# Weight tiles with even and odd columns in separate halves, streamed in turn by the matmuls

## The chip, the core and the metric

The kernel runs on one core of one Trainium2 chip. A core has a matrix engine (PE), which reads both operands from on-chip memory (SBUF, 128 partitions) and writes to PSUM, and four more engines: DVE (VectorE), ACT (ScalarE), POOL (GpSimd) and SP (SyncE, which here only issues DMAs). Each runs its own list of instructions in order; semaphores join them. The metric is the time of one execution in microseconds of device time (us); lower is better.

## The reference

Two layers of a decoder trunk on 256 tokens of width 1024, batch 1, all in float32. Each layer is a SwiGLU block of inner width 2816, a mixer of three gated branches (short convolution, sparse attention, attention to 256 memory tokens), and a second SwiGLU block, each between two RMS norms:

```python
def swiglu(h, w_in, w_out):
    a, b = jnp.split(h @ w_in, 2, axis=-1)
    return (jax.nn.silu(a) * b) @ w_out

for l in range(DEPTH):
    h = rms_norm(x, ffn1_norm_pre[l])
    x = x + 0.5 * rms_norm(swiglu(h, ffn1_w_in[l], ffn1_w_out[l]), ffn1_norm_post[l])
    h = rms_norm(x, mix_norm_pre[l])
    y = token_mixer(h, mem, cos, sin, ...)
    x = x + rms_norm(y, mix_norm_post[l])
    h = rms_norm(x, ffn2_norm_pre[l])
    x = x + 0.5 * rms_norm(swiglu(h, ffn2_w_in[l], ffn2_w_out[l]), ffn2_norm_post[l])
```

What matters here is that nearly all of the work is a product of a 128-token block of activations with a large float32 weight matrix: `w_in` (1024 x 5632), `w_out` (2816 x 1024), the mixer's input projection (1024 x 6424) and its smaller matrices.

## The kernel before

The tokens are two blocks of 128 (`stream(0)` and `stream(1)`), and both walk through the same list of steps, the second a few steps behind. The weights come from memory once, in units of up to 512 KB: 1024 float32 words on each of 128 partitions (128 rows by 1024 columns, or two blocks of rows by 512, or four by 256). A unit takes three steps before a matmul can use it:

- `load` (line 244) issues a DMA from SP into one of 4 tiles `raw`.
- `split_unit` (line 280) makes two tiles of it, out of 8 pairs: ACT rounds `raw` to the matrix engine's type float32r and writes `whi` (line 286), and DVE subtracts, `wlo = raw - whi` (line 287). `prefetch` (line 293) calls it up to 4 steps ahead of the use.
- the matmuls take three products for each block of 128 rows: `whi` with the high part of the activations, `wlo` with the high part, and `whi` with the low part. The activations are the stationary operand (`lhsT`, loaded by LDWEIGHTS, 128 columns), and the weights are the moving operand (`rhs`), which streams through the array: 512 columns in most matmuls.

The moving operand is a plain slice of the tile, 512 neighbouring words on each partition. These places use it: `product` (line 356, the SwiGLU input in two banks), `mm3` (lines 344 to 346) through `product2` (mixer, branches, memory, and the tail of the SwiGLU input) and through `output` (line 528), and `compress` (lines 956 and 958, 256 columns). `mm3` is also called with operands that are no weight units (`mem_attention`, `compress`).

`view(ap, off, dims)` (line 104) builds an access pattern by hand: a list of [step, count] pairs in words, the outermost first, the partition left as it is.

In the profile `acc`, `y` and `br` are PSUM banks, `hThi`/`hTlo`, `turnhi`/`turnlo` and `mThi`/`mTlo` are high and low parts of activations. The order on each engine is a fixed list that the program's walk writes out; no table is touched here.

Of the kernel before, what the change touches and what calls it, by code (L numbers as in the profile page):

```python
# [103 lines left out]
def view(ap, off, dims):  # L104
    if isinstance(ap, Nothing):
        return ap
    return bass.AP(tensor=ap.tensor, offset=ap.offset + off, ap=[list(ap.ap[0])] + [list(d) for d in dims])


def f32(ap):  # L110
    return ap.bitcast(F32)
# [19 lines left out]
def program(tc, nc, pools, a, out, plan):  # L131
# [18 lines left out]
    def bank(name):  # L150
        return psa.tile([P, 512], F32, name=name, tag="a")
# [4 lines left out]
    def gtile(name, dt=F32):  # L156
        return gp.tile([P, 1024], dt, name=name, tag="g")
# [17 lines left out]
    def pinned(ins):  # L175
        if first_steps[0] and not dry:
            tc.keep_in_program_order(ins)
# [3 lines left out]
    first = consts.tile([16, P], F32, name="first")  # L181
    nc.scalar.dma_start(first, a[PRE[0]].rearrange("l (k p) -> (l k) p", p=P))
    for half in range(2):
        sl = slice(half * 512, (half + 1) * 512)
# [45 lines left out]
    def unit(key, parts):  # L230
        hi, lo = ask("w", key, parts)
        later(0, lambda: drop("w", key))
        return hi, lo
# [46 lines left out]
    def split_unit(between=None):  # L280
        item, raw, n = splits.pop(0)
        free["w"] -= 1
        hi = wp.tile([P, 1024], F32R, name="whi")
        lo = wp.tile([P, 1024], F32R, name="wlo")
        for c0, c1 in ((0, n),) if between is None else ((0, n // 2), (n // 2, n)):
            pinned(nc.scalar.copy(hi[:, c0:c1], raw[:, c0:c1]))  # L286
            pinned(nc.vector.tensor_sub(lo[:, c0:c1], raw[:, c0:c1], f32(hi[:, c0:c1])))  # L287
            if c0 == 0 and between is not None:
                between()
        ready[item[2]] = [hi, lo]  # L290
        free["raw"] += 1

    def prefetch():
        if dry:
            return
        ahead = AHEAD if now[0] > RAMP else 1
        while splits and splits[0][0][0] <= now[0] + ahead and free["w"] > 0:
            split_unit()
        if now[0] == 0 and not prologue:
            prologue.append(True)  # L300
            load(loads.pop(0), (nc.sync, nc.scalar))
            load(loads.pop(0))
            nc.sync.dma_start(x[1], a["x"][0, P:2 * P, :])
        room = {"raw": True, "g": True}
        for item in list(loads):
            if item[0] > now[0] + LOADS or not any(room.values()):
                break
            kind = "g" if item[1] == "g" else "raw"
            room[kind] = room[kind] and free[kind] > 0
            if room[kind]:  # L310
                load(item)
                loads.remove(item)

    def fetch(key):
        while key not in ready:
            if splits and (splits[0][0][2] == key or free["raw"] == 0):
                split_unit()
            else:
                item = loads.pop(0)
                if item[1] == "g" and item[2] != key:  # L320
                    raise RuntimeError(f"no room for {key} before {item[2]}")
                load(item)
                if item[1] != "g":
                    continue
# [14 lines left out]
    if not dry:  # L339
        loads.extend(plan)  # L340
        left.update({item[2]: item[4] for item in plan})

    def mm3(ps, xh, xl, wh, wl, start, stop, skip=False):
        nc.tensor.matmul(ps, lhsT=xh, rhs=wh, start=start, stop=False, skip_group_check=skip)  # L344
        nc.tensor.matmul(ps, lhsT=xh, rhs=wl, start=False, stop=False, skip_group_check=skip)  # L345
        nc.tensor.matmul(ps, lhsT=xl, rhs=wh, start=False, stop=stop, skip_group_check=skip)  # L346

    def product(hT, name, l, cols):
        ps = [bank("acc") for _ in cols]
        for k in range(8):  # L350
            parts = [(0, -1, name, l, k, 1, cols[0][0], cols[0][1])]
            hi, lo = unit((name, l, cols[0][0], k), parts)
            for i, (x2, w) in enumerate(((0, hi), (1, hi), (0, lo))):
                for j, p in enumerate(ps):
                    n = cols[j][1]
                    pinned(nc.tensor.matmul(p[:, :n], lhsT=hT[x2][:, k], rhs=w[:, j * n:(j + 1) * n],  # L356
                                            start=(k == 0 and i == 0), stop=(k == 7 and i == 2)))
            yield 0
        return ps

    def product2(ps, x2, hi, lo, n, k0, first, last):
        for kk in range(2):
            k = k0 + kk
            mm3(ps[:, :n], x2[0][:, k], x2[1][:, k], hi[:, kk * n:(kk + 1) * n], lo[:, kk * n:(kk + 1) * n],
                first and kk == 0, last and kk == 1)

    def halves(hT, name, l, parts):
        ps = bank("acc")
        width = sum(n for _, n in parts)
        for u in range(4):  # L370
            hi, lo = unit((name, l, parts[0][0], u), [(i * n, width, name, l, 2 * u, 2, c, n)
                                                      for i, (c, n) in enumerate(parts)])
            product2(ps, hT, hi, lo, width, 2 * u, u == 0, u == 3)
            yield 0
        return ps
# [70 lines left out]
    def prenorm(src, name, l, warm=False):  # L446
# [18 lines left out]
        if warm and splits:  # L465
            pts = []
            for half in range(2):
                pts.append(transpose4(src, half * 512))
                keep_clock(WARM[1 + half])
            gained(0, pts[0])  # L470
            split_unit(lambda: halved(0))
            split_unit()
            gained(1, pts[1])
            halved(1)
        else:
            for half in range(2):
                gained(half, transpose4(src, half * 512))
            for half in range(2):
                halved(half)
# [36 lines left out]
    def output(y, name, l, count, lhs, between=None):  # L516
        steps = [[(k, 0), (k, 1)] for k in range(count)]
        if TAIL:
            steps[-TAIL:] = [[(k, 0)] for k in range(count - TAIL, count)]
            steps[-1] += [(k, 1) for k in range(count - TAIL, count)]  # L520
        for n, step in enumerate(steps):
            if between is not None:
                between(n)
            for k, i in step:
                hi, lo = unit((name, l, k), [(0, 0, name, l, k, 1, 0, 1024)])
                sl = slice(i * 512, (i + 1) * 512)
                xh, xl = lhs(k)
                mm3(y[i], xh, xl, hi[:, sl], lo[:, sl], k == 0, k == count - 1)
            yield 0


    def ffn(t, l, which):
# [15 lines left out]
        for j in range(5):  # L548
            pa, pb = yield from product(hT, w_in, l, [(j * 512, 512), (DFF + j * 512, 512)])
            gate(j, 512, pa, pb)  # L550
# [7 lines left out]
        def lhs(k):  # L558
            c = (k % 8) * P
            return [v[:, c:c + P] for v in gT[k // 8]]  # L560

        yield from output(y, w_out, l, 22, lhs, between)
        yield from postnorm(y, t, (f"ffn{which}_norm_post", l, t), 0.5, which == 2 and l == DEPTH - 1)

# [365 lines left out]
    def compress(l, i):  # L930
# [13 lines left out]
        FHL = gtile("FHL", F32R)  # L944
# [4 lines left out]
        z = bank("z")  # L949
        w1 = f"cmp_{nm}_w1"  # L950
        for u in range(4):
            hi, lo = unit((w1, l, u), [(0, 256, w1, l, 4 * u, 4, 0, 256)])
            for mm in range(4):
                m = 4 * u + mm
                c = mm * 256
                nc.tensor.matmul(z[0:64, 0:256], lhsT=FHL[:, m * 64:(m + 1) * 64], rhs=hi[:, c:c + 256],  # L956
                                 start=(m == 0), stop=False, skip_group_check=True)
                nc.tensor.matmul(z[0:32, 0:256], lhsT=FHL[:, m * 64:m * 64 + 32], rhs=lo[:, c:c + 256],  # L958
                                 start=False, stop=(m == 15), skip_group_check=True)
            yield 1  # L960
        nc.scalar.copy(zc[0:64], z[0:64, 0:256])
# [17 lines left out]
        if i == 0:  # L979
# [11 lines left out]
            ps = bank("kc")  # L991
            for ht in range(2):
                h2, l2 = wh[:, ht].rearrange("p a d -> p (a d)"), wl[:, ht].rearrange("p a d -> p (a d)")
                mm3(ps[:, 0:32], h2, l2, gh[:, ht], gl[:, ht], ht == 0, ht == 1)
# [3 lines left out]
        else:  # L998
# [11 lines left out]
            ps = bank("vc")  # L1010
# [204 lines left out]
    def mixer(t, l):  # L1215
# [11 lines left out]
        def squeeze():  # L1227
            for i in range(2):
                add(("cmp", l), compress(l, i))
# [68 lines left out]
        def between(k):  # L1298
            if k == SECOND:
                transpose_half(1)  # L1300

        yield from output(y, "w_mix_out", l, 8, lambda k: (mT[0][:, k], mT[1][:, k]), between)
        yield from postnorm(y, t, ("mix_norm_post", l, t), 1.0)

# [73 lines left out]
```

## Time and profile before

| | |
|---|---|
| median of 3 runs (lowest to highest) | 1254.22 us (1254.11 to 1254.84) |
| span of the profiled execution, first to last instruction | 1252.2 us |
| instructions | 16623 |
| DMA, mean over the span | 229 GB/s, 286.85 MB |

The profile shows one execution of the program. The span leaves out what lies before the first instruction and after the last one; the profiled execution's own time is not listed apart from the three runs, whose median is 2.0 us above its span. Busy times of PE overlap, since a matmul's end is modelled and the next one starts before it; what a matmul costs in a dense stretch is therefore read from start to start in the timeline and not from its duration. DVE and ACT rows can be read as they stand.

### The profile page before, as it was taken

What the parts mean: (1) busy time and instruction counts of PE and PEld (TensorE: products, weight loads), DVE (VectorE), ACT (ScalarE), POOL (GpSimd) and SP (SyncE); (2) the same over time, 40 slices, a digit from 0 to 9 for tenths busy, and PEclk for the clock granted to TensorE, in tenths of its full rate; (3) what the DMA queues carried; (4) which work ended last, traced back from release to release, by engine and by line L of the source; (5) the groups of instructions that cost most, each with busy time, mean ns of one, the idle gap of its engine ahead of it and who ended that gap; (6) DMA issues with size and microseconds to landing.
All of it is one profiled execution on the core that took longest, in us unless ns stands there. A gap on an engine that the chain in (4) does not pass through costs nothing.

```text
span 1252.2 us, 16623 instructions
## 1 busy us (share of the span) xinstructions
PE 1239.9 (99%) x5775; PEld 1027.1 (82%) x5775; DVE 911.3 (73%) x1160; ACT 729.5 (58%) x1146; POOL 209.6 (17%) x413
## 2 busy tenths in 40 slices
PE   8999999999999999999999999999999999999997
PEld 6888888888888888888888888878888888888886
DVE  7766766888988686666576676678899976757752
ACT  6545545887866454544464555569868744545541
POOL 3011601401120011011011014023022200110110
PEclk9999999999999999999999999999999999999999
DMA  7878876777578757776857788757667877577871
GB/s 254 261 244 260 280 250 221 215 238 217 182 264 252 219 179 210 247 255 218 260 177 224 237 269 295 246 177 245 213 185 236 281 223 218 180 241 219 257 244 70
DMA packets 133907, 286.85 MB, mean 229 GB/s; under 512 B 11872, under 2 KB 30976, under 8 KB 133824
## 3 DMA queue, kind: packets, MB, share of 16 engines
q1 hardware_dynamic: 117984, 238.78, 60.6%
q0 software_dynamic: 15520, 46.49, 11.3%
q8 instruction: 45, 0.74, 0.2%
q10 hardware_dynamic: 320, 0.53, 0.1%
q14 instruction: 38, 0.31, 0.1%
HBM read 261.64 MB, written 24.12 MB: 228 GB/s over the span
## 4 chain that ended last, share of the span: by engine, by line
PE 93%; DVE 2%; DMA 1%; ACT 1%; issue 1%; POOL 1%; SPq 0%; DVEq 0%; POOLq 0%; ACTq 0%
PE acc L356 35%; PE acc L346 9%; PE acc L344 9%; PE acc L345 9%; PE y L345 7%; PE y L346 7%; PE y L344 7%; PE pt L388 2%; PE br L344 2%; PE br L345 2%; PE br L346 2%; DMA x<-in_x_dram 1%; PE z L958 1%; PE s L917 1%; PE z L956 1%
## 5 line engine op out<-in xcount | busy, mean ns | idle before, releaser
L287 DVE TENSOR_TENSOR wlo<-raw,whi 128x1024 fp32r<-128x1024 f32 (+2 forms) x441 | 532.1, 1213 | 244.8 <-ACT whi L286 240.8
L286 ACT CAST whi<-raw 128x1024 fp32r<-128x1024 f32 (+2 forms) x441 | 456.4, 1043 | 362.5 <-PE acc L356 182.0
L356 PE MATMUL acc<-wlo,hThi 128*128 128x512 f32 x640 | 198.4, 390 | 0.0
L356 PE MATMUL acc<-whi,hThi 128*128 128x512 f32 x640 | 197.9, 390 | 0.5 <-ACT whi L286 0.5
L356 PE MATMUL acc<-whi,hTlo 128*128 128x512 f32 x640 | 197.2, 389 | 0.0
L344 PE MATMUL acc<-whi,hThi 128*128 128x512 f32 (+1 forms) x480 | 188.2, 392 | 0.4 <-ACT hThi L462 0.4
L345 PE MATMUL acc<-wlo,hThi 128*128 128x512 f32 (+1 forms) x480 | 184.8, 385 | 0.0
L346 PE MATMUL acc<-whi,hTlo 128*128 128x512 f32 (+1 forms) x480 | 184.6, 385 | 0.2
L403 POOL DMA_DIRECT2D there<-blocks x184 | 101.2, 556 | 492.3 <-DVE blocks L398 407.5
L356 PEld LDWEIGHTS acc<-whi,hThi 128*128 128x128 f32 x640 | 119.7, 188 | 25.7 <-ACT whi L286 0.8
L356 PEld LDWEIGHTS acc<-whi,hTlo 128*128 128x128 f32 x640 | 120.0, 188 | 25.2 <-DVE hTlo L463 0.3
L356 PEld LDWEIGHTS acc<-wlo,hThi 128*128 128x128 f32 x640 | 120.0, 188 | 25.2 <-DVE wlo L287 0.4
L346 PE MATMUL y<-whi,turnlo 128*128 128x512 f32 x352 | 137.3, 390 | 0.0
L345 PE MATMUL y<-wlo,turnhi 128*128 128x512 f32 x352 | 137.2, 390 | 0.0
L344 PE MATMUL y<-whi,turnhi 128*128 128x512 f32 x352 | 137.1, 389 | 0.0
L346 PEld LDWEIGHTS acc<-whi,hTlo 128*128 128x128 f32 x480 | 90.1, 188 | 18.7 <-DVE hTlo L463 0.6
L344 PEld LDWEIGHTS acc<-whi,hThi 128*128 128x128 f32 x480 | 90.3, 188 | 17.1 <-ACT hThi L462 1.3
L345 PEld LDWEIGHTS acc<-wlo,hThi 128*128 128x128 f32 x480 | 90.4, 188 | 15.0
L344 PEld LDWEIGHTS y<-whi,turnhi 128*128 128x128 f32 x352 | 66.1, 188 | 13.8
L346 PEld LDWEIGHTS y<-whi,turnlo 128*128 128x128 f32 x352 | 66.1, 188 | 13.6
L345 PEld LDWEIGHTS y<-wlo,turnhi 128*128 128x128 f32 x352 | 66.1, 188 | 13.6
L424 DVE TENSOR_TENSOR turnlo<-moved,turnhi 128x1024 fp32r<-128x1024 f32 (+1 forms) x42 | 49.2, 1171 | 33.1 <-ACT turnhi L423 33.0
(294 smaller groups left out, 1451.4 us busy)
## 6 DMA issues: line engine op xcount, KB each, us to landing
raw<-in_ffn_w_in_dram SPq DMA_DIRECT2D x159, 512.0 KB, 4.8
raw<-in_w_mix_in_dram SPq DMA_DIRECT2D x96, 512.0 KB, 4.7
raw<-in_ffn_w_out_dram SPq DMA_DIRECT2D x88, 512.0 KB, 4.6
there<-blocks POOLq DMA_DIRECT2D x152, 128.0 KB, 4.4
moved<-there POOLq DMA_DIRECT2D x38, 512.0 KB, 5.2
raw<-in_ffn_w_in_dram SPq DMA_DIRECT2D x33, 256.0 KB, 4.1
raw<-in_w_mem_kv_dram SPq DMA_DIRECT2D x16, 512.0 KB, 4.7
raw<-in_w_mix_out_dram SPq DMA_DIRECT2D x16, 512.0 KB, 4.0
```

The costliest lines, as they stand in the source:

```text
L286: pinned(nc.scalar.copy(hi[:, c0:c1], raw[:, c0:c1]))
L287: pinned(nc.vector.tensor_sub(lo[:, c0:c1], raw[:, c0:c1], f32(hi[:, c0:c1])))
L344: nc.tensor.matmul(ps, lhsT=xh, rhs=wh, start=start, stop=False, skip_group_check=skip)
L345: nc.tensor.matmul(ps, lhsT=xh, rhs=wl, start=False, stop=False, skip_group_check=skip)
L346: nc.tensor.matmul(ps, lhsT=xl, rhs=wh, start=False, stop=stop, skip_group_check=skip)
L356: pinned(nc.tensor.matmul(p[:, :n], lhsT=hT[x2][:, k], rhs=w[:, j * n:(j + 1) * n], start=(k == 0 and i == 0), stop=(k == 7 and i == 2)))
L388: pinned(nc.tensor.transpose(pt[:, j * P:(j + 1) * P], src[:, c0 + j * P:c0 + (j + 1) * P], ident))
L403: nc.gpsimd.dma_start(there[:, q * f:(q + 1) * f].rearrange("(p j) f -> j p f", j=32), blocks[q * 32:(q + 1) * 32, :n].rearrange("j (p f) ...
L424: nc.vector.tensor_sub(lv, mv, f32(hv))
L917: nc.tensor.matmul(s3[:, i], lhsT=QT[:, g * 4 + u * 2 + i], rhs=KT[j][:, var * 2 + g], start=(i == 0 and j == 0), stop=(i == 1 and j == 1) ...
L956: nc.tensor.matmul(z[0:64, 0:256], lhsT=FHL[:, m * 64:(m + 1) * 64], rhs=hi[:, c:c + 256], start=(m == 0), stop=False, skip_group_check=True)
L958: nc.tensor.matmul(z[0:32, 0:256], lhsT=FHL[:, m * 64:m * 64 + 32], rhs=lo[:, c:c + 256], start=False, stop=(m == 15), skip_group_check=True)
```

## The change

A helper `moving` builds a pattern that takes one word from the lower half of a 1024-word tile, then the word 512 further on, then the next of the lower half, and so on. `split_unit` reads `raw` with a step of two words: first the even columns, which it writes to the lower half of `whi` and `wlo`, then the odd columns, which go to the upper half. The matmuls that have weight units as moving operand read them through `moving`, so the columns come out in the same order as before. A new `mm3w` wraps `mm3` for them; matmuls of other operands stay as they are. The number of instructions, their order and their waits are the same on all five engines.

```diff
+def moving(w, c, n):
+    return view(w, c // 2, [[1, n // 2], [512, 2]])
...
         for c0, c1 in ((0, n),) if between is None else ((0, n // 2), (n // 2, n)):
-            pinned(nc.scalar.copy(hi[:, c0:c1], raw[:, c0:c1]))
-            pinned(nc.vector.tensor_sub(lo[:, c0:c1], raw[:, c0:c1], f32(hi[:, c0:c1])))
+            source = view(raw, c0, [[1, 2], [2, (c1 - c0) // 2]])
+            h2, l2 = (view(v, c0 // 2, [[512, 2], [1, (c1 - c0) // 2]]) for v in (hi, lo))
+            pinned(nc.scalar.copy(h2, source))
+            pinned(nc.vector.tensor_sub(l2, source, f32(h2)))
...
+    def mm3w(ps, xh, xl, hi, lo, c, n, start, stop):
+        mm3(ps, xh, xl, moving(hi, c, n), moving(lo, c, n), start, stop)
...
-                    pinned(nc.tensor.matmul(p[:, :n], lhsT=hT[x2][:, k], rhs=w[:, j * n:(j + 1) * n],
+                    pinned(nc.tensor.matmul(p[:, :n], lhsT=hT[x2][:, k], rhs=moving(w, j * n, n),
...
-            mm3(ps[:, :n], x2[0][:, k], x2[1][:, k], hi[:, kk * n:(kk + 1) * n], lo[:, kk * n:(kk + 1) * n],
-                first and kk == 0, last and kk == 1)
+            mm3w(ps[:, :n], x2[0][:, k], x2[1][:, k], hi, lo, kk * n, n, first and kk == 0, last and kk == 1)
...
-                sl = slice(i * 512, (i + 1) * 512)
                 xh, xl = lhs(k)
-                mm3(y[i], xh, xl, hi[:, sl], lo[:, sl], k == 0, k == count - 1)
+                mm3w(y[i], xh, xl, hi, lo, i * 512, 512, k == 0, k == count - 1)
...
-                nc.tensor.matmul(z[0:64, 0:256], lhsT=FHL[:, m * 64:(m + 1) * 64], rhs=hi[:, c:c + 256],
+                nc.tensor.matmul(z[0:64, 0:256], lhsT=FHL[:, m * 64:(m + 1) * 64], rhs=moving(hi, c, 256),
...
-                nc.tensor.matmul(z[0:32, 0:256], lhsT=FHL[:, m * 64:m * 64 + 32], rhs=lo[:, c:c + 256],
+                nc.tensor.matmul(z[0:32, 0:256], lhsT=FHL[:, m * 64:m * 64 + 32], rhs=moving(lo, c, 256),
```

## The prediction, made before the changed kernel was run

> **What bounds the kernel now.** I began with the page: busy shares, the slices of the span, the chain that ended last.
>
> ```profile
> PE 1239.9 (99%) x5775; PEld 1027.1 (82%) x5775; DVE 911.3 (73%) x1160; ACT 729.5 (58%) x1146; POOL 209.6 (17%) x413
> PEclk9999999999999999999999999999999999999999
> PE 93%; DVE 2%; DMA 1%; ACT 1%; issue 1%; POOL 1%; SPq 0%; DVEq 0%; POOLq 0%; ACTq 0%
> ```
>
> The matrix engine is busy for 99% of the 1252.2 us span, at full granted clock in every slice, and the chain is 93% PE. No wait is left to remove; the time is the number of matmuls times their spacing. The spacing is in the timeline of PE, here a stretch of the SwiGLU output (start, duration, instruction):
>
> ```profile
> 599.43 0.39 PE L344 MATMUL y<-whi,turnhi 128*128 128x512 f32 x1
> 599.66 0.39 PE L345 MATMUL y<-wlo,turnhi 128*128 128x512 f32 x1
> ...
> 611.90 0.39 PE L345 MATMUL y<-wlo,turnhi 128*128 128x512 f32 x1
> ```
>
> From 599.43 to 611.90 there are 55 spacings: 12.47 / 55 = 0.2267 us for 512 columns, 0.443 ns a column. The listed 390 ns is latency and overlaps. The count of 512-column matmuls that stream weights comes from the groups, first of the page and then of the groups kept apart by shape:
>
> ```profile
> L356 PE MATMUL acc<-whi,hThi 128*128 128x512 f32 x640 | 197.9, 390 | 0.5 <-ACT whi L286 0.5
> L344 PE MATMUL y<-whi,turnhi 128*128 128x512 f32 x352 | 137.1, 389 | 0.0
> ```
>
> ```profile
> L344 PE MATMUL acc<-whi,hThi 128*128 128x512 f32 x448 | 178.6, 399 | 0.4 <-ACT hThi L462 0.4
> L344 PE MATMUL y<-whi,mThi 128*128 128x512 f32 x64 | 25.3, 396 | 0.0
> L344 PE MATMUL acc<-whi,mThi 128*128 128x512 f32 x64 | 24.9, 389 | 0.0
> L344 PE MATMUL br<-whi,ynsa 128*128 128x512 f32 x32 | 12.6, 395 | 0.0
> ```
>
> Each group stands for three products: 3 x (640 + 352 + 448 + 64 + 64 + 3 x 32) = 4992, the last term being the three branches. At 0.2267 us they fill 1132 us, 90% of the span. So one nanosecond of spacing is worth 5.0 us, and whatever the new pattern does to the stream decides the case.
>
> **The stream: is there anything to gain?** I look for a second point on the line of spacing against columns. Matmuls of 256 columns with 128 columns of weights:
>
> ```profile
> 322.90 0.28 PE L1122 MATMUL om<-turnhi,vm 128*128 128x256 f32 x1
> ...
> 324.34 0.40 PE L344 MATMUL acc<-whi,hThi 128*128 128x512 f32 x1
> ```
>
> ```profile
> 325.73 0.28 PE L917 MATMUL s<-KTh,QT 128*128 128x256 f32 x1
> 325.84 0.28 PE L917 MATMUL s<-KTl,QT 128*128 128x256 f32 x1
> 325.96 0.28 PE L917 MATMUL s<-KTh,QT 128*128 128x256 f32 x1
> ```
>
> Twelve matmuls of L1122 take 1.44 us, 120 ns each, so the second 256 columns of a 512-column matmul cost 226.7 - 120 = 106.7 ns, 0.417 ns a column against the mean of 0.443. At that rate alone 512 columns are 213.3 ns, 13.4 ns less than now. That is the most the rows allow a better stream to gain. Whether the 13.4 ns belongs to the words or to each matmul is what the rows of L917 bear on: the first of those starts only 0.11 us before the next, so 256 columns can pass in 113 ns or so, half of 227. A fixed 13 ns for each matmul would have forbidden that. So I read the excess as a pause that comes every so many words of a contiguous float32r stream, and such a pause is something that another order of words can remove. Two half-tiles in turn make two streams, each with twice the time per word. For a loss there are rows too, taken up with the rivals.
>
> [...]
>
> **The split: what the step of two costs.** 441 units go through one ACT and one DVE instruction each, whose input now has a step of two words and whose output is two runs of 512. The rows:
>
> ```profile
> L287 DVE TENSOR_TENSOR wlo<-raw,whi 128x1024 fp32r<-128x1024 f32 x431 | 524.8, 1225 | 243.6 <-ACT whi L286 239.7
> L286 ACT CAST whi<-raw 128x1024 fp32r<-128x1024 f32 x431 | 450.2, 1052 | 360.1 <-PE acc L356 182.0 <-PE y L346 79.3 <-PE acc L346 52.5
> L424 DVE TENSOR_TENSOR turnlo<-moved,turnhi 128x1024 fp32r<-128x1024 f32 x34 | 41.6, 1222 | 20.3 <-ACT turnhi L423 20.2
> L463 DVE TENSOR_TENSOR hTlo<-hf,hThi 128x512 fp32r<-128x512 f32 x24 | 15.9, 687 | 0.6 <-ACT hThi L462 0.5
> L942 DVE TENSOR_TENSOR F<-G,smallT 128x240 f32<-128x240 f32 x8 | 4.3, 583 | 0.0
> ```
>
> L424 reads its first input in runs of 32 words with jumps between them and costs 1222 ns against 1225: jumps as such are free. L942 reads its first input with a step of 16 words. From 512 and 1024 columns (687 and 1225 ns) a contiguous column costs 1.05 ns and an instruction 149 ns, so 240 columns would be 401 ns; 583 is 182 more, 0.76 ns a column. So the two ends for the split are 0 and 1024 x 0.76 = 776 ns an instruction, for DVE 441 x 0.776 = 342 us in all. ACT has no row with a step; I take the same two ends. I choose 0, because a step of two is one doubling from a run and three from the step of 16. At this value the cover isn't even needed: in front of the splits DVE idles 243.6 us for ACT, and ACT 360.1 us mostly for PE to release a pair. If the price were the upper end, that cover holds in the SwiGLU stages only (rival C).
>
> [...]
>
> **What faster matmuls bring late.** The stages differ, in busy time of PE, PEld, DVE, ACT, POOL per 100 us:
>
> ```profile
> 200.00:300.00 100.00, 99.56 (x540) 84.14 (x539) 84.78 (x137) 80.83 (x175) 23.23 (x41) 1.00 0.70 215
> 300.00:400.00 100.00, 99.89 (x481) 82.77 (x480) 89.38 (x142) 72.90 (x147) 18.10 (x36) 1.00 0.71 226
> 500.00:600.00 100.00, 100.00 (x443) 82.81 (x442) 64.67 (x63) 47.30 (x51) 13.97 (x26) 1.00 0.75 239
> 800.00:900.00 100.00, 99.57 (x525) 83.84 (x525) 79.28 (x112) 75.12 (x152) 21.05 (x37) 1.00 0.71 224
> 900.00:1000.00 100.00, 99.27 (x496) 83.01 (x495) 90.94 (x163) 77.61 (x170) 22.33 (x42) 1.00 0.72 225
> ```
>
> In the SwiGLU stages (500 to 600) DVE and ACT have a third and more to spare, and DMA is at 0.75 of its engines' time; 5% more speed asks 0.79. In the mixers DVE is at 85 to 91%. The full gain would be 66.9 / 1252.2, 5.3 us in 100, which puts DVE at 94 to 96% in two of the windows, where a queue of dependent steps starts to show. I count nothing of the gain in those two (300 to 400 and 900 to 1000): 2 x 5.3 = 11 us given back. The ends for this term are 0 and four windows, 21 us.
>
> **The sum.** Profiled span 1252.2. Stream of the 512-column matmuls: -4992 x 13.4 ns = -66.9. The 128 matmuls of 256 columns in `compress` and the 96 of 280 gain at most half as much each, 224 x 7 ns = -1.6. Split: 0. Given back in the mixers: +11. That is 1194.7; with the 2.0 us by which the median of the runs (1254.22) stands above the span, 1196.7: **1197 us**. The likeliest case's own range is from 1186 (nothing given back) to 1222 (half of the stream's gain, 1252.2 - 34.3 + 2.0 = 1220, and a little for the split).
>
> **Rivals.** A is the forecast.
>
> B, the pause stays: the 13.4 ns is spent between matmuls (change of weights), or alternation pauses as often as a contiguous stream does. Then nothing moves and the change doesn't do what it could: 1254 us. For it: the straight line through 120 and 226.7 has just such a fixed part. Against it: the 0.11 us of L917.
>
> C, the split pays the step: DVE at 776 ns more for each unit. The DVE time of the splits alone in the mixer windows:
>
> ```profile
> 200.00:300.00 100.00, 45.53 (x39) 1.00 0.70 215
> 300.00:400.00 100.00, 35.72 (x30) 1.00 0.71 226
> 800.00:900.00 100.00, 46.77 (x40) 1.00 0.71 224
> 900.00:1000.00 100.00, 34.96 (x29) 1.00 0.72 225
> ```
>
> 39, 30, 40 and 29 splits add 30.3, 23.3, 31.0 and 22.5 us, so DVE needs 115, 113, 110 and 113 us in each 100: 51 us over, and DVE is the bound there. With an unchanged stream that is 1305 us; with A's stream, whose gain then counts only outside these windows (850 of 1252 us, 46 us), 1259. Slower either way. For it: L942. Against it: its step is 16, not 2.
>
> D, the stream itself stalls, and the change is much slower. The place is the PE's read of the moving operand: if it fetches neighbouring words together and uses both, then an order that leaves a neighbour behind with every column halves what a fetch yields. Two words a fetch means twice the spacing, 453 ns, +226.7 ns x 4992 = +1132 us: 2386 us. With the extra that L942 shows on DVE, 0.76 ns a column, it is 512 x 0.76 = 389 ns each, +1942 us: 3196 us. It decides from the first nanosecond that a column costs above 0.443. For it: L942 shows that SBUF reads of single words can cost 1.81 ns a column, four times what PE takes now. Against it: L942 never comes back to a neighbour, while here each half is read word by word in order, and every neighbour is used two columns later, if the reader holds two places at once.
>
> [...]
>
> **How the numbers follow.** Chances: A 0.52, B 0.16, C 0.12, D 0.20. A leads because the excess over 0.417 ns looks like one of words and because two ordered streams aren't single-word hops. D is as large as it is because no row shows the pattern. The range takes in A, B and C, from 1184 to 1312, and leaves out D, whose price is far off. A measurement here tells about 0.2%, 2.5 us, from no change: faster is A, 0.52; within is B, 0.16; slower is C and D, 0.32.
>
> **What would show it.** A: in the changed profile the 55 spacings of such a stretch are 213 to 216 ns, L286 and L287 stay at 1052 and 1225 ns, and PE shows its first idle time in the mixers, with ACT or DVE as releaser. B: 227 again. C: L287 near 2000 ns, DVE at full in the mixers, PE waiting for `wlo`. D: spacings of 450 ns and more with PE still at 99% and DVE idle. I am wrong most plainly if the spacing rises, since every other term is small beside it.

## The result, and the profile after

| | before | changed |
|---|---|---|
| median (lowest to highest), 4 runs each | 1254.16 us (1253.99 to 1254.84) | 1265.59 us (1259.27 to 1269.44) |
| ratio to before, 95% interval | | 1.0085 (1.0057 to 1.0113) |
| span of the profiled execution | 1252.2 us | 1257.6 us |
| mean granted PE clock of that execution | 0.998 | 0.992 |

The changed kernel is slower by 0.9%. The profiled execution is the fastest of its four, so the profile shows 5.4 of the 11.4 us between the medians. The page of the changed kernel, busy times and granted clock:

```profile
PE 1197.1 (95%) x5775; PEld 1035.6 (82%) x5775; DVE 1018.1 (81%) x1160; ACT 930.1 (74%) x1146; POOL 214.8 (17%) x413
PEclk9999989999999999999999999999999999999999
```

PE is busy 42.8 us less than before (1239.9), and idle for 1257.6 - 1197.1 = 60.5 us where it was 12.3: 48.2 us more. Two large terms nearly cancel. DVE and ACT together do 307 us more. The timeline of PE in a dense stretch of the changed kernel (start, duration, instruction):

```profile
544.81 0.38 PE L365 MATMUL acc<-whi,hThi 128*128 128x512 f32 x1
...
556.68 0.60 PE L365 MATMUL acc<-whi,hTlo 128*128 128x512 f32 x2
```

Between these two starts lie 55 spacings: 11.87 / 55 = 0.2158 us each, where it was 0.2267. So the stream gained 10.9 ns a matmul, 54 us over 4992 of them. The groups of the changed kernel by shape (busy, mean ns, idle time before them) show where it went:

```profile
L292 ACT CAST whi<-raw 128x1024 fp32r<-128x1024 f32 x431 | 656.7, 1546 | 165.8 <-PE acc L365 67.6 <-PE acc L355 20.9 <-DMA raw<-in_ffn_w_in_dram 20.7
L293 DVE TENSOR_TENSOR wlo<-raw,whi 128x1024 fp32r<-128x1024 f32 x431 | 639.4, 1496 | 148.4 <-ACT whi L292 145.9 <-PE acc L365 1.6
L431 ACT CAST turnhi<-moved 128x1024 fp32r<-128x1024 f32 x34 | 35.9, 1055 | 33.5 <-DMA moved<-there 33.3
```

The copy costs 1546 ns where it was 1052 (+494), the subtraction 1496 where it was 1225 (+271), in the 431 units of 1024 columns. A copy of the same size with other operands, L431, still costs about what it did (1055, 1046 before). What PE waited for in the changed kernel (total us, times, longest):

```profile
PE pt L396 <- DVE x L519: 7.6, 10, 1.0
PE pt L396 <- DVE v L1145: 7.0, 4, 2.6
PE acc L353 <- ACT mThi L673: 6.9, 3, 5.3
PE zt L972 <- ACT zc L968: 4.2, 2, 2.1
PE br L353 <- DVE gth L1298: 3.8, 2, 3.3
...
PE acc L365 <- DVE wlo L293: 0.3, 1, 0.3
```

Almost nothing waits for the weight tiles themselves (0.3 us for `wlo`). PE waits for other short work of DVE and ACT, which share their queues with the splits: the residual, the convolution's product, scores, gates. That it is the splits that hold these up is read from the order of the queues; a run below, with the same stream and cheaper splits, shows it better. The longest wait, 5.3 us for `mThi`, has a DMA in its chain: DVE waited up to 4.3 us for the tile `moved` before it. The windows of the changed kernel (busy time of PE, PEld, DVE, ACT, POOL, then clock, DMA share and GB/s) say where:

```profile
100.00:200.00 100.00, 92.14 (x409) 79.59 (x408) 72.24 (x63) 63.48 (x55) 29.22 (x52) 0.95 0.76 254
200.00:300.00 100.00, 90.31 (x503) 78.22 (x502) 83.47 (x116) 87.28 (x165) 21.58 (x36) 1.00 0.67 206
300.00:400.00 100.00, 94.74 (x485) 81.91 (x484) 95.00 (x155) 83.62 (x150) 22.12 (x42) 1.00 0.71 220
500.00:600.00 100.00, 100.00 (x465) 87.70 (x464) 78.96 (x68) 67.86 (x52) 16.54 (x30) 1.00 0.77 249
800.00:900.00 100.00, 93.73 (x500) 81.16 (x499) 80.61 (x96) 84.15 (x129) 22.16 (x37) 0.98 0.70 217
900.00:1000.00 100.00, 91.54 (x485) 80.32 (x484) 92.74 (x163) 84.75 (x176) 17.96 (x33) 1.00 0.67 207
```

In the SwiGLU stage from 500 to 600 the plan holds: PE is full and issues 465 matmuls where it issued 443. In the four mixer windows PE is at 90 to 95%: 29.7 us of idle time, where it was 1.7. From 100 to 200 the granted clock is 0.95 beside 8 us of idle time; before it was 1.00 in every such window. In steps of 5 us, two stretches of idle time there and the clock behind them (the same columns):

```profile
145.00:150.00 5.00, 2.41 (x11) 1.76 (x11) 3.12 (x5) 4.95 (x8) 3.80 (x7) 0.94 0.45 146
150.00:155.00 5.00, 5.00 (x18) 4.16 (x17) 4.11 (x5) 2.24 (x2) 4.74 (x8) 0.72 0.92 325
175.00:180.00 5.00, 0.78 (x2) 0.69 (x3) 3.13 (x3) 1.04 (x1) 0.00 (x0) 0.67 0.29 109
180.00:185.00 5.00, 5.00 (x17) 4.08 (x16) 0.95 (x2) 1.91 (x2) 0.00 (x0) 0.65 0.32 105
```

PE passes 18 and 17 matmuls in the full step right after the gap, at clocks of 0.72 and 0.65, and 25 in the dense steps around it. How long a gap it takes is not settled by this trace: from 265 to 270 PE is busy for 3.19 of the 5 us, and the clock is 1.00 there and in the full step behind it; from 880 to 885 it is busy for 2.76, and the clock is 0.83 there and in the step behind it. Over the span, 0.998 - 0.992 is 0.006 x 1257.6, by estimate at most 8 us, since some of it falls on idle time. The four runs move with it: 1259.3 us at 0.992, 1265.3 and 1265.9 at 0.988, 1269.4 at 0.987. The stream's 54.4 us less, 48.2 us more of idle time and these 8 us add up to 2 us more; the spans differ by 5.4, so some 4 us stay unexplained.

### The profile page after: what moved, and what is told of

Same layout as the page of the kernel before. It is cut to its first block, busy times and chain, and to the rows that moved or that the text cites. A ratio compares the mean times of both kernels' runs of the same rounds, so it can differ in the third digit from the quotient of the medians.

```text
span 1257.6 us, 16623 instructions
## 1 busy us (share of the span) xinstructions
PE 1197.1 (95%) x5775; PEld 1035.6 (82%) x5775; DVE 1018.1 (81%) x1160; ACT 930.1 (74%) x1146; POOL 214.8 (17%) x413
## 3 DMA queue, kind: packets, MB, share of 16 engines
q0 software_dynamic: 15520, 46.49, 11.4%
## 5 line engine op out<-in xcount | busy, mean ns | idle before, releaser
L292 ACT CAST whi<-raw 128x1024 fp32r<-128x1024 f32 (+2 forms) x441 | 665.3, 1531 | 167.8 <-PE acc L365 67.6
L293 DVE TENSOR_TENSOR wlo<-raw,whi 128x1024 fp32r<-128x1024 f32 (+2 forms) x441 | 647.5, 1481 | 149.9 <-ACT whi L292 147.4
L365 PE MATMUL acc<-whi,hThi 128*128 128x512 f32 x640 | 191.7, 381 | 2.1 <-DVE wide L551 1.7
L365 PE MATMUL acc<-wlo,hThi 128*128 128x512 f32 x640 | 191.9, 380 | 0.3 <-DVE wlo L293 0.3
L365 PE MATMUL acc<-whi,hTlo 128*128 128x512 f32 x640 | 190.8, 380 | 0.9 <-DVE hTlo L471 0.9
L353 PE MATMUL acc<-whi,hThi 128*128 128x512 f32 (+1 forms) x480 | 183.4, 382 | 0.7 <-ACT hThi L470 0.7
L355 PE MATMUL acc<-whi,hTlo 128*128 128x512 f32 (+1 forms) x480 | 179.9, 375 | 0.5 <-DVE hTlo L471 0.5
L354 PE MATMUL acc<-wlo,hThi 128*128 128x512 f32 (+1 forms) x480 | 179.8, 375 | 0.0
L355 PE MATMUL y<-whi,turnlo 128*128 128x512 f32 x352 | 134.6, 382 | 0.0
L431 ACT CAST turnhi<-moved 128x1024 fp32r<-128x1024 f32 (+1 forms) x42 | 42.5, 1013 | 58.8 <-DMA moved<-there 55.8
```

Of the source, the lines that this page charges most:

```text
L292: pinned(nc.scalar.copy(h2, source))
L293: pinned(nc.vector.tensor_sub(l2, source, f32(h2)))
L365: pinned(nc.tensor.matmul(p[:, :n], lhsT=hT[x2][:, k], rhs=moving(w, j * n, n), start=(k == 0 and i == 0), stop=(k == 7 and i == 2)))
L431: nc.scalar.copy(hv, mv)
```

## The experiments

The theory after the result was that the stream gains and the step of two costs the copies, each by itself. The first two runs take the change apart. Both feed the matmuls columns in another order and so compute other numbers, with the same instructions and sizes.

**The stream alone.** The split of before, the matmuls of the change (in the few units of 560 columns the halves are 280 words apart):

```diff
-            source = view(raw, c0, [[1, 2], [2, (c1 - c0) // 2]])
-            h2, l2 = (view(v, c0 // 2, [[512, 2], [1, (c1 - c0) // 2]]) for v in (hi, lo))
-            pinned(nc.scalar.copy(h2, source))
-            pinned(nc.vector.tensor_sub(l2, source, f32(h2)))
+            pinned(nc.scalar.copy(hi[:, c0:c1], raw[:, c0:c1]))
+            pinned(nc.vector.tensor_sub(lo[:, c0:c1], raw[:, c0:c1], f32(hi[:, c0:c1])))
```

> The split as before (contiguous), the matmuls streaming the two halves in turn as in the change. The columns of every weight tile reach the matmuls in another order, so the numbers computed are others; every instruction, size and wait is the change's. Theory (the stream gains, the split's step of two costs): spacing of 512-column matmuls 216 ns as in the changed profile, ACT's copy back at 1052 ns and DVE's subtraction at 1225 ns, PE idle under 15 us, time 1198 to 1206 us. Rival (the slower copies come from the PE's reads in turn, which disturb ACT and DVE): the copy stays near 1546 ns and the subtraction near 1496 ns, and the time stays near 1260 us.

Measured: 1219.96 us (1211.16 to 1227.91), ratio 0.9723 (0.9669 to 0.9777). PE's timeline, 23 spacings of 216 ns, and the groups of this kernel:

```profile
599.77 0.38 PE L352 MATMUL y<-wlo,turnhi 128*128 128x512 f32 x1
...
604.73 0.38 PE L351 MATMUL y<-whi,turnhi 128*128 128x512 f32 x1
```

```profile
L290 ACT CAST whi<-raw 128x1024 fp32r<-128x1024 f32 x431 | 447.3, 1047 | 299.7 <-PE acc L363 148.1 <-PE y L353 57.0 <-PE acc L353 41.3
L291 DVE TENSOR_TENSOR wlo<-raw,whi 128x1024 fp32r<-128x1024 f32 x431 | 523.3, 1223 | 194.8 <-ACT whi L290 190.7 <-PE acc L363 1.3
```

The stream's gain is real, and PE's reads in turn don't disturb a contiguous copy (1047 ns, 1052 before): that rival falls. The time is 14 us above the upper end of what was expected, and PE idles for 1214.9 - 1187.8 = 27.1 us where under 15 were expected. The split is as cheap here as before, so a faster stream alone loses about 20 of its 54 us (1219.96 against 1254.2 - 54.4); the windows of the mixers, further below, bear on that.

**The split alone.** The split of the change, contiguous matmuls:

```diff
 def moving(w, c, n):
-    return view(w, c // 2, [[1, n // 2], [512, 2]])
+    return view(w, c // 280 * 512 if n == 280 else c, [[1, n]])
```

> The split with the step of two as in the change, the matmuls reading contiguous words as before (columns in another order, so other numbers). Theory: spacing 227 ns, ACT's copy 1546 ns, DVE's subtraction 1496 ns, and a time above before by less than the 51 us of rival C in the prediction, since DVE rises by 0.27 us a unit and not 0.78: 1262 to 1275 us. Rival (PE's reads in turn slow the copies): copy 1052 ns, subtraction 1225 ns, time 1254 us.

Measured: 1259.01 us, ratio 1.0040 (1.0025 to 1.0055). The groups:

```profile
L292 ACT CAST whi<-raw 128x1024 fp32r<-128x1024 f32 x431 | 481.0, 1123 | 337.7 <-PE acc L365 167.6 <-PE y L355 75.1 <-PE acc L355 51.3
L293 DVE TENSOR_TENSOR wlo<-raw,whi 128x1024 fp32r<-128x1024 f32 x431 | 524.8, 1224 | 246.8 <-ACT whi L292 243.2
```

Neither answer fits, and the time lies between the two that were expected. The step of two costs ACT 71 ns a copy (1123, 1052 before) and DVE nothing (1224, 1225 before); the 1546 and 1496 ns need both halves of the change at once. So the theory of two separate terms falls too. For a whole unit the two runs of 512 words lie end to end, so that in the kernel before, the changed one and these two the split writes the same places in the same order: on its side only the order in which it reads `raw` differs. The trace of the changed kernel has the same answer inside it. Two of its copies, and what PE did meanwhile:

```profile
318.56 1.54 ACT L292 CAST whi<-raw 128x1024 fp32r<-128x1024 f32 x1
...
321.92 0.63 PE L396 MATMUL pt<-ident,v 128*128 128x128 f32 x4 [1.65 <-DVE v L1145]
321.96 1.21 ACT L292 CAST whi<-raw 128x1024 fp32r<-128x1024 f32 x1
322.30 0.46 PE L353 MATMUL acc<-whi,hThi 128*128 128x512 f32 x1
...
322.60 0.60 PE L1063 MATMUL pt<-ident,pc 128*96 128x128 f32 x4
```

The copy at 318.56 lies beside an unbroken stream in turn and takes 1.54 us; the one at 321.96 lies beside transposes, which read word after word, for more than half of its time, and takes 1.21. The new theory: reads of SBUF with a step of two and PE's reads in turn collide. The word stands here for what was measured, a copy of 1546 ns with both where it is 1123 with the first alone and 1047 with the second; what happens inside the memory no run shows.

**Other ways to take turns.** Runs of two words instead of one, and the jump on the writing side of the split instead of the reading side.

```diff
-    return view(w, c // 2, [[1, n // 2], [512, 2]])
+    return view(w, c // 2, [[2, n // 4], [512, 2], [1, 2]])
...
-            source = view(raw, c0, [[1, 2], [2, (c1 - c0) // 2]])
-            h2, l2 = (view(v, c0 // 2, [[512, 2], [1, (c1 - c0) // 2]]) for v in (hi, lo))
+            m = (c1 - c0) // 4
+            source = view(raw, c0, [[2, 2], [4, m], [1, 2]])
+            h2, l2 = (view(v, c0 // 2, [[512, 2], [2, m], [1, 2]]) for v in (hi, lo))
```

> As the change, but in runs of two words: the split reads two neighbouring words and skips two, the matmuls take two words of one half, then two of the other; columns in the right order. If a lone word is what costs the split, its copies go back to 1052 and 1225 ns. If the stream's gain needs a change of half at every column, the spacing goes back to 227 ns, and the time is 1254 us; if a change at every second column is enough, the spacing is 216 ns and the time 1198 to 1206 us. By the theory that the gain comes from two ordered streams, 216 ns is the likelier.

Measured: 1775.43 us, ratio 1.4153 (1.4132 to 1.4174). The timeline of PE, 18 matmuls from the first start to the last, 344 ns each there (about 328 in other stretches of the trace):

```profile
599.56 0.58 PE L354 MATMUL y<-whi,mThi 128*128 128x512 f32 x1
...
605.75 0.51 PE L354 MATMUL y<-whi,mThi 128*128 128x512 f32 x1
```

Turns at every second word are much worse than no turns at all. Neither spacing that was expected came, and the one called likelier, 216 ns, is far off: two ordered streams by themselves don't make the gain. The copy costs 1150 ns and the subtraction 1224, near what they cost beside contiguous matmuls (1123 and 1224); since both patterns changed at once, this doesn't tell which of them the collision needs. A stall of the stream is what rival D of the prediction warned of, but its reason doesn't fit: runs of two leave no neighbour behind, and it is they that lose, while single words gain.

```diff
-            h2, l2 = (view(v, c0 // 2, [[512, 2], [1, (c1 - c0) // 2]]) for v in (hi, lo))
-            source = view(raw, c0, [[1, 2], [2, (c1 - c0) // 2]])
+            h2, l2 = (view(v, c0 // 2, [[1, (c1 - c0) // 2], [512, 2]]) for v in (hi, lo))
+            source = view(raw, c0, [[2, (c1 - c0) // 2], [1, 2]])
```

> As the change, but the split reads raw word after word and writes (and DVE reads whi) in turn to the two halves; the same tiles result. If only a step of two words in the input costs, the copy is 1052 ns and the subtraction 1225 ns, and the time is 1198 to 1206 us. If a lone word costs on the writing side too, the copy stays above 1400 ns, the subtraction rises above 1496 ns since two of its three operands now jump, and the time is above the change's 1265 us.

Measured: 1419.13 us, ratio 1.1309 (1.1290 to 1.1328). The groups:

```profile
L293 DVE TENSOR_TENSOR wlo<-raw,whi 128x1024 fp32r<-128x1024 f32 x431 | 913.0, 2191 | 92.3 <-ACT whi L292 89.5 <-PE acc L365 1.7 <-ACT kk L627 0.2
L292 ACT CAST whi<-raw 128x1024 fp32r<-128x1024 f32 x431 | 905.4, 2192 | 116.3 <-DMA raw<-in_ffn_w_in_dram 42.0 <-DMA raw<-in_ffn_w_out_dram 19.3 <-PE acc L355 10.0
```

The second answer came: jumps at every word are dearer on the writing side. How much of this is the collision is not shown. By estimate the two copies of 512 columns take 1.1 us each in this run (all 441 copies at 2169 ns less 431 at 2192 and 8 at 1203); the first of them takes 0.66 us in the changed kernel, where it ends before PE reads any weights.

**Four words.** The same edit as with pairs, with 4 for 2.

> As the change, but in runs of four words of one half, then four of the other. Two readings of the 216 and 328 ns seen so far. Reading 1 (PE reads the even and the odd columns of a stream as two streams, and each runs the better the more neighbouring words it gets before it jumps): with four, even and odd columns each get two words of a half before a jump, as in a contiguous read they get two of every four, so the spacing is between 216 and 328 ns, near 227. Reading 2 (any jump but one at every column costs, the more the rarer): above 227 ns by half of what pairs added, about 277 ns. The copies stay near 1150 and 1224 ns by both, since PE no longer reads in turn.

Measured, in a single run: 1365.39 us beside 1254.43. 25 spacings in 6.25 us of the timeline are 250 ns each:

```profile
599.72 0.67 PE L366 MATMUL acc<-wlo,hThi 128*128 128x512 f32 x2
...
605.97 0.42 PE L356 MATMUL acc<-whi,hTlo 128*128 128x512 f32 x1
```

That lies between the two readings (227 and 277), so neither is shown. The copy costs 1071 ns (near 1150 was expected), the subtraction 1224. The four patterns stand at 216 (one word in turn), 227 (no turns), 250 (four) and 328 to 344 ns (two). What PE does inside to make this order stays open.

**The distance of the halves.** If two kinds of read collide, the place should matter. The upper half is moved by 4 words, and in another run by 32 (distance 544, tiles of 1056 words):

```diff
-    return view(w, c // 2, [[1, n // 2], [512, 2]])
+    return view(w, c // 2, [[1, n // 2], [516, 2]])
...
-        hi = wp.tile([P, 1024], F32R, name="whi")
-        lo = wp.tile([P, 1024], F32R, name="wlo")
+        hi = wp.tile([P, 1028], F32R, name="whi")
+        lo = wp.tile([P, 1028], F32R, name="wlo")
...
-            h2, l2 = (view(v, c0 // 2, [[512, 2], [1, (c1 - c0) // 2]]) for v in (hi, lo))
+            h2, l2 = (view(v, c0 // 2, [[516, 2], [1, (c1 - c0) // 2]]) for v in (hi, lo))
```

> As the change, but the upper half begins 516 words after the lower one and not 512. Theory (the copies are slow because their reads with a step of two and the PE's reads in turn meet in the same part of SBUF): another distance spreads the PE's two reads, the copy falls from 1546 ns toward 1123 ns, where it stood with a contiguous PE stream, and the time falls to between 1220 and 1250 us; spacing 216 ns. Rival (the two kinds of read share a total rate, wherever they go): copy and subtraction stay at 1500 to 1550 and 1480 to 1500 ns, time 1260 to 1270 us.

> As the run with 516, at a distance of 544 words (512 + 32). The same two answers: copy toward 1123 ns and time 1220 to 1250 us if the place matters; 1500 to 1550 ns and 1260 to 1270 us if only the rate does.

Measured: at 516 words 1220.58 us, ratio 0.9739 (0.9713 to 0.9766); at 544 words 1225.45 us, 0.9754 (0.9719 to 0.9790). The groups at 516:

```profile
L292 ACT CAST whi<-raw 128x1024 fp32r<-128x1024 f32 x431 | 495.7, 1161 | 271.4 <-PE acc L365 132.4 <-PE y L355 42.7 <-PE acc L355 41.9
L293 DVE TENSOR_TENSOR wlo<-raw,whi 128x1024 fp32r<-128x1024 f32 x431 | 523.6, 1224 | 201.6 <-ACT whi L292 198.3
```

The collision is gone but for some 40 ns of ACT's copy (1161 against 1123), the stream stays at 216 ns (6.26 us for 29 spacings), and the kernel beats the one before by 2.6%. PE's waits shrink with it: for the residual `x` from 7.6 to 1.6 us, for `v` from 7.0 to 4.3, for `mThi` from 6.9 to 2.0. A rival is left: wider tiles move everything that lies behind them. The control has the width of 516 and the distance of 512:

```diff
-        hi = wp.tile([P, 1024], F32R, name="whi")
-        lo = wp.tile([P, 1024], F32R, name="wlo")
+        hi = wp.tile([P, 1028], F32R, name="whi")
+        lo = wp.tile([P, 1028], F32R, name="wlo")
```

> The control to the runs with 516 and 544: the tiles are 1028 words wide as with 516, so every tile behind them lies where it lay there, but the upper half begins at word 512 as in the change. Theory (the distance of the two halves decides): the copy is at 1546 ns and the subtraction near 1496 ns, time 1259 to 1270 us. Rival (the width moved the tiles against raw, and that took the collision away): copy 1161 ns, subtraction 1224 ns, time 1218 to 1228 us.

Measured: 1264.02 us, ratio 1.0060 (1.0041 to 1.0079). The groups:

```profile
L292 ACT CAST whi<-raw 128x1024 fp32r<-128x1024 f32 x431 | 650.8, 1534 | 168.3 <-PE acc L365 79.5 <-PE acc L355 21.1 <-DMA raw<-in_ffn_w_in_dram 16.5
L293 DVE TENSOR_TENSOR wlo<-raw,whi 128x1024 fp32r<-128x1024 f32 x431 | 638.4, 1495 | 149.4 <-ACT whi L292 146.5 <-PE acc L365 1.4
```

It is the distance, and not the width of the tiles. The same tiles at 514 words:

> As the run with 516, at a distance of 514 words (8 bytes more than 512 words), in tiles of 1028. If places are 16 bytes or more wide, the two reads of PE share a place for half of the words, and the copy is between 1161 and 1546 ns, near 1350 ns, time 1235 to 1255 us. If they are 8 bytes wide, 514 is as good as 516: copy 1161 ns, time 1218 to 1228 us.

Measured: 1247.74 us, ratio 0.9950 (0.9928 to 0.9972); the copy 1414 ns, the subtraction 1391. Two words of shift take part of the collision away, four take all that 32 take (1161 ns in both). Of the two answers the first is nearer, though the copy is 64 ns above the 1350 that it expected; the second, 1161 at 514 words too, did not come. That the memory has places of such a width was an assumption of the author's, and no run shows it.

**No step in the split at all.** The columns can also be put in order behind PSUM. The split stays contiguous, the matmuls of the SwiGLU input (but for its tail of 256 columns) and of the output projections take the two halves of their own 512 words in turn, and the readers of those banks take every second column:

```diff
+def moving(w, c, n):
+    return view(w, c, [[1, n // 2], [n // 2, 2]])
...
+def apart(ps, n):
+    return view(ps, 0, [[1, 2], [2, n // 2]])
+def joined(ap, c, n):
+    return view(ap, c, [[n // 2, 2], [1, n // 2]])
...
+            t2 = th[:, :n] if j == 5 else joined(th, 0, n)
+            a2, b2 = (p[:, :n] if j == 5 else apart(p, n) for p in (pa, pb))
-            nc.scalar.activation(th[:, :n], pa[:, :n], AF.Tanh, scale=r_half)
+            nc.scalar.activation(t2, a2, AF.Tanh, scale=r_half)
...
-            nc.vector.scalar_tensor_tensor(tmp[i][:, :512], y[i], 32.0 * factor, g[:, sl], op0=OP.mult, op1=OP.mult)
+            nc.vector.scalar_tensor_tensor(joined(tmp[i], 0, 512), apart(y[i], 512), 32.0 * factor,
+                                           joined(g, i * 512, 512), op0=OP.mult, op1=OP.mult)
```

> A version that keeps the split of before (contiguous) and takes the columns in turn only in the SwiGLU input and in the two output projections: the two halves of a 512-column slice, 256 words apart; the results then lie in turn in PSUM, and the few instructions that read those banks put them back in order with a step of two. 3168 matmuls of 512 columns in turn. Theory: their spacing is 216 ns, 34.5 us less; copies at 1050 and 1225 ns; the readers of PSUM (144 instructions of 512 columns or so) cost at most 0.3 us more each, mostly beside PE: time 1220 to 1232 us. Rival (PSUM reads with a step cost as the split's did, about 0.5 us, and hold up the chain of the gates): 1240 us and more.

Measured: 1224.58 us, ratio 0.9778 (0.9750 to 0.9805). The matmuls in turn, with halves 256 words apart, last 380 to 381 ns in the mean, as with 516 (380 to 381, at a spacing of 216), where the same groups took 389 to 390 before; the contiguous copy stays at 1048 ns. The readers of PSUM (busy, mean ns), which took 746, 686, 684 and 684 ns before:

```profile
L559 DVE SCALAR_TENSOR_TENSOR wide<-th,rs,acc 128x512 f32<-128x512 f32 x40 | 29.8, 746 | 2.3
L553 ACT ACTIVATE th<-acc,rs 128x512 f32<-128x512 f32 x40 | 27.4, 684 | 7.7 <-PE acc L368 7.4
L554 DVE SCALAR_TENSOR_TENSOR th<-th,acc 128x512 f32<-128x512 f32 x40 | 27.3, 682 | 0.6 <-ACT th L553 0.6
L518 DVE SCALAR_TENSOR_TENSOR pn<-y,gB 128x512 f32<-128x512 f32 x24 | 16.3, 684 | 10.7 <-ACT junk L446 10.7
```

A step of two on a PSUM read costs nothing here (at most 2 ns of difference in the four groups), less than was allowed for.

**Both ways at once.** SwiGLU and output units as in the last run, all others with halves 516 words apart:

```diff
             h2, l2, source = hi[:, c0:c1], lo[:, c0:c1], raw[:, c0:c1]
+            if not item[3][0][2].startswith("ffn") and item[3][0][2] != "w_mix_out":
+                source = view(raw, c0, [[1, 2], [2, (c1 - c0) // 2]])
+                h2, l2 = (view(v, c0 // 2, [[516, 2], [1, (c1 - c0) // 2]]) for v in (hi, lo))
...
```

> Both ways at once: the SwiGLU units and the output projections are split contiguously and put in order behind PSUM, the mixer's, branches', memory's and compression's units are taken with a step of two into halves 516 words apart. All streams in turn but the tail of the SwiGLU input. Theory (what is left over 1199 us is lost in the mixers, where DVE is at 90% and more, whatever the split costs elsewhere): spacing 216 ns, no gain over the run with 516: 1214 to 1226 us. Rival (ACT's 113 ns a unit more, against a contiguous split, costs time): 1205 to 1213 us.

Measured: 1225.49 us (1220.12 to 1225.80), ratio 0.9753 (0.9729 to 0.9777). Its copy is down to 1100 ns and the time is no better than with 516 alone, whose interval overlaps. With copies of 1047 (the stream alone), 1100 and 1161 ns (516) the times are 1220, 1225 and 1221 us: what ACT spends on the split no longer decides. The windows of the run with 516 show what is left:

```profile
200.00:300.00 100.00, 96.63 (x552) 84.84 (x551) 87.46 (x150) 85.05 (x178) 23.47 (x43) 1.00 0.70 213
300.00:400.00 100.00, 98.94 (x490) 85.57 (x489) 92.24 (x138) 77.64 (x147) 17.34 (x32) 1.00 0.73 236
800.00:900.00 100.00, 95.44 (x544) 83.29 (x543) 84.53 (x148) 82.92 (x174) 24.89 (x45) 1.00 0.69 212
900.00:1000.00 100.00, 95.58 (x469) 82.89 (x469) 89.11 (x134) 76.21 (x146) 16.50 (x31) 0.98 0.72 227
```

PE now idles 13.4 us in these four windows (1.7 before). The full gain would bring 1254.4 - 54.4 = 1200 us; some 20 us are lost. In the profiled execution PE's idle time is 13.8 us above that of before and its busy time falls by 49.3 us and not by 54.4, so most of the loss is these waits, and the rest lies in the busy time, beside a clock of 0.996.

## Why the prediction was wrong

The forecast was faster, 1197 us; the kernel got slower, 1265.6.

- **The bound** was right: PE's spacing decides first, and 4992 matmuls of it.
- **The stream** was right in sign and near in size. It was taken at 213.3 ns, -66.9 us; it measured 215.8 ns, 54.4 us, 12.5 less. Rival B falls: the stream alone took the kernel to 0.9723. The reasons given are not confirmed. The 0.11 us of L917 is one spacing at the timeline's step of 0.01 us; the four there (325.73 to 326.20) are 118 ns in the mean, nearer to 120 than to 113, so that a fixed share was not ruled out. The 256-column matmuls of `compress` went from 117 to 109 ns (seven spacings, 0.82 and 0.76 us), more than half of the 10.9 ns of 512 columns, so the gain does not go by the words alone. And the runs of two words show that two ordered streams can also lose. That the order of the words would gain at all was in part luck.
- **The split at 0 is the step that failed**, and not for the reason weighed there. "I choose 0, because a step of two is one doubling from a run and three from the step of 16" is about right for the edit by itself: +71 ns on ACT, 0 on DVE. What failed is that the two edits were costed apart. With PE reading in turn at a distance of 512 words, the same copy costs +494 and the same subtraction +271 ns. Against the run with the stream alone, which differs from the changed kernel in the split, this term is 1265.6 - 1220.0 = 46 us of the 69 by which the forecast was off. The bounds from L942 (0 to 776 ns) held the number; the choice inside them rested on a row that ran beside contiguous matmuls, as every row of before does.
- **The term given back in the mixers** was 11 us for an unchanged split. The stream alone, with such a split, loses about 20 us against its full gain, near the term's upper end of 21, and so does the run with 516, where the two mixer windows that the term left out (200 to 300 and 800 to 900, DVE at 87 and 85%) have 3.4 and 4.6 us of idle time; so waits show below the 94 to 96% from which the term counted them. With the dear split of the change, PE's idle time rose by 48.2 us, and the granted clock fell beside it.
- **Rival C** named the right place, a dearer split that fills DVE and ACT in the mixers, and with A's stream put it at 1259 us. Its mechanism was wrong: it charged the step, while the step and the stream together are charged. That its number lies near the measured one is luck. Two of its signs failed: L293 is at 1496 ns, not near 2000, and PE waits 0.3 us in all for `wlo`. A third came in part: DVE is at 95 and 93% in two of the four mixer windows, at 83 and 81% in the others.
- **Rival D** did not happen for the pattern of the change. A stalling stream exists, for runs of two words, at 1.4 times the time, but not for the reason that D gave.
- **The range**, 1184 to 1312, holds the time only because it took in rival C, whose mechanism is not what happened.

## What to carry to other kernels

Cost the access patterns of engines that run side by side together and not one by one, and if a pattern that costs little alone (71 ns a copy here) costs much beside another (494), shift one operand by 16 bytes before giving it up: here that turned a loss of 0.9% into a gain of 2.6%. Where PE is at 99%, the spacing of its matmuls is the place to look, and a different order of the moving words was worth 5% of it here. Where another engine is nearly full in a stage, part of a faster stream can be lost in waits: with DVE at 79 to 91% in the mixers, some 20 of 54 us went, though the split cost no more than before.

## What the runs showed that was not expected

- A contiguous float32r stream costs 226.7 ns for 512 columns; the same words read in turn from two places cost 215.8 at a distance of 512 words and 216 at 516 (at 256 and 544 the mean durations, 380 to 382 ns in the SwiGLU and output groups, are within 2 ns of those at 516); in turns of two words, 512 apart, 328 to 344, of four 250.
- ACT copies with a step of two: 1123 ns beside contiguous matmuls, 1546 beside reads in turn 512 words apart, 1414 at 514, 1161 at 516 and 544. A contiguous copy beside reads in turn 512 apart: 1047. So only the pair of patterns collides, and of the four distances only 2048 bytes, and in part 2056, do it. Why these distances and not the others, no run shows.
- Reading PSUM with a step of two costs ACT and DVE nothing (682 to 746 ns for 512 columns, as before).
- Writing to two halves in turn costs ACT 2192 ns for 1024 columns beside PE's reads in turn, more than reading with a step of two does there (1546).
